# A two-layer transformer block on one core: the first layer's last conditioning vector loaded during the first mixer, four more FFN column blocks by seven products, and one fixed order from the mixer's output into the FFN

## The chip, the core and the metric

The kernel runs on one core of a Trainium2 chip, in one launch. A core has five engines with instruction streams of their own: TensorE (PE, with its weight loads shown apart as PEld), VectorE (DVE), ScalarE (ACT), GpSimd (POOL) and SyncE (SP), which here issues the loads from device memory. Each engine works through its stream in order and waits on semaphores of the others. The metric is the device time of the launch in microseconds (us), smaller is better.

## The reference, cut to what matters

All in float32: 512 tokens, width 1024, two layers. Layer 0 mixes the tokens with a gated linear recurrence (`hgrn2_mixer`), layer 1 with dilated attention. Each mixer is followed by a SwiGLU feed-forward network (FFN) with inner width 2816.

```python
cond = jax.nn.silu(c)
for layer in range(DEPTH):                               # DEPTH = 2
    mod = (cond @ ada_w[layer] + ada_b[layer])[:, None, :]      # 1024 -> 6 * 1024
    sh1, sc1, g1, sh2, sc2, g2 = jnp.split(mod, 6, axis=-1)
    u = rms_norm(h, norm_g[layer, 0]) * (1.0 + sc1) + sh1
    y = hgrn2_mixer(u, ...) if layer % N_MIXERS == 0 else dilated_attention_mixer(u, ...)
    h = h + (1.0 + g1) * rms_norm(y, norm_g[layer, 1])
    u = rms_norm(h, norm_g[layer, 2]) * (1.0 + sc2) + sh2
    gate, up = jnp.split(u @ ffn_w_in[layer], 2, axis=-1)       # 1024 -> 2 * 2816
    y = (jax.nn.silu(gate) * up) @ ffn_w_out[layer]             # 2816 -> 1024
    h = h + (1.0 + g2) * rms_norm(y, norm_g[layer, 3])
```

The six vectors of a layer are called (layer, 0) to (layer, 5) below; (0, 5) is `g2` of layer 0, which is needed only after the first FFN.

## The kernel before, in words

**Split operands.** Every large product is taken in three passes: each operand is kept as a high part and a low part, and `three` (L400 to L404) adds high·high, low·high and high·low into one PSUM bank. ACT makes a high part by a copy into the reduced format, DVE makes the low part by a subtraction. A matmul covers 128 rows of the contraction and up to 512 columns.

**The stream of weights.** One list `items` fixes the order in which all weights are loaded and split (class `Stream`). An item lands in a tile "raw" of 1 MB, of which there are two; SP issues the load of the next item as soon as a raw tile has been read for the last time. Items of kind "w" are split by ACT (L83) and DVE (L84), or piecewise by `pieces` (L104, L105). Items "ada" are quarters of a conditioning vector's weights: vectors (0, 2) to (0, 4) go through PE (`ada_groups`, L221, with the tile `tiled_cond`), all others through DVE as one multiplication and seven multiply-adds for each half (L241, L243) and a sum across partitions on POOL (L245). Items "rows" carry bias and norm rows and finish a gate vector (`row_fin`, L290, L291). Items "quarters" are the four quarters of an FFN block. `weave` mixes the conditioning items into the weights. Before the change (0, 5) stands among the first eight FFN weights.

**The FFN.** The 2816 inner columns are 22 blocks of 128. `PLAIN` gives the number of pairs of blocks that are computed plainly: four in layer 0 and two in layer 1. A plain block takes 48 matmuls of 512 columns for gate and up together. The other blocks go through `seven_products`: by a seven-product scheme over a 2 x 2 cut of weights and tokens, a block takes seven runs of twelve matmuls with 256 columns each. That needs four sums of quarters of the FFN's input, split into `th` and `tl`; `token_sums` makes them: on DVE four additions (L711), four further combinations (L712 to L715) and four subtractions (L718), on ACT four copies (L717).

**Mixer output and entry into the FFN.** `mixer_out` multiplies by the mixer's output weights, normalises (class `Turn`: `gated`, `r_y` and `r_h` for the reciprocal roots on POOL, `upds` for the residual, `xn`, `flip` for the transposes on PE, `u_of` and `parts_of` for the split FFN input `uh`, `ul`), and starts the first pair of plain blocks, two token halves one after the other (`half`; the second half's first lines are L670 and L673). Its four PSUM banks `pss` are handed to `ffn`, where SiLU on ACT (L876) reads two of them and a multiplication on DVE (L877) the other two. The next pair uses the same four banks of tag "mm" again: its first matmul waits for the first SiLU of the pair before, in both programs.

**What sets the order.** Inside `tc.manual_schedule` the instructions of PE, ACT, DVE and POOL keep the written order. Elsewhere a scheduler places them. The last part of `mixer_out` and all of `seven_products` stand in such blocks; what `ffn` does between the two is placed by the scheduler, which may put it between instructions of the fixed blocks.

Of the kernel before, what the change touches and what calls it, by code (L numbers as in the profile page):

```python
# [15 lines left out]
P = 128  # L16
S = 512
# [133 lines left out]
def block_kernel(tc, x, c, positions, ada_w, ada_b, norm_g, hgrn_w_in, lower, hgrn_norm_g, hgrn_w_out,  # L151
# [6 lines left out]
    with ExitStack() as ctx:  # L158
# [14 lines left out]

        pre = ctx.enter_context(ExitStack())
# [34 lines left out]
        tiled_cond = []  # L209
        by_pe = lambda l, v: l == 0 and v in (2, 3, 4)  # L210

        def ada_groups(l, v, hf, kq):


            def run(raw):
                if kq == 0:
                    accs[l, v, hf] = bank("mm")
                ps, r = accs[l, v, hf], V4(raw)
                for k in range(4):
                    j = slice(32 * k, 32 * k + 32)  # L220
                    pe.matmul(ps[j], tiled_cond[0][:, kq * 4 + k], r[:, k], start=kq == 0, stop=kq == 1,  # L221
                              tile_position=(0, 32 * k))
                if kq == 1:
                    accs[l, v, hf] = acc_place()
                    act.copy(accs[l, v, hf], ps)
            return run
# [84 lines left out]


# [29 lines left out]
        PLAIN = (4, 2)  # L342
# [10 lines left out]
        items += weave(hg, ada_seq((0, 2), (0, 4), (0, 3)), 1)  # L353
        items += hg_o
        f0a, f0b = ffn_ws(0)
        n0 = 2 * PLAIN[0]
        items += weave(f0a[:n0], ada_seq((0, 5)), 2, 1) + f0a[n0:]
# [61 lines left out]
        turns = ctx.enter_context(ExitStack())  # L419

# [84 lines left out]
        def mixer_out(oT, otp, groups, gate, l, side, close, tail=None):  # L505
# [69 lines left out]
            n = Turn(side, y0, y1, gate, (l, 1))  # L575

            with tc.manual_schedule(engines=ORDERED):
                (hi_a, lo_a), (hi_b, lo_b) = st.pieces(2)
                n.sq_y(0, 0)
                n.gated(0, 0)  # L580
                mm(0, range(8) if tail is None else (7,))
                n.sq_y(0, 1)
                n.gated(0, 1)
                n.r_y(0)
                n.sq_y(1, 0)
                n.gated(1, 0)
                n.sq_y(2, 0)
                n.upds(0)
                n.sq_y(3, 0)
                n.gated(2, 0)  # L590
                n.r_h(0)
                hi_a()
                n.xn(0)
                mm(1, range(8))
                n.sq_y(1, 1)
                n.gated(1, 1)
                n.r_y(1)
                n.gated(3, 0)
                hi_b()
                n.upds(1)  # L600
                lo_a()
                mm(2, range(4))
                n.flip(0, [bank("b"), bank("b")])
                n.u_of(0, 0)
                n.r_h(1)
                n.u_of(0, 1)
                n.parts_of(0, 0)
                n.xn(1)
                n.parts_of(0, 1)
                lo_b()  # L610
                st.fill()
                mm(3, range(4))
                (hi_a, lo_a), (hi_b, lo_b) = st.pieces(2)
                mm(2, range(4, 6))
                n.flip(1, [bank("b"), bank("b")])
                n.u_of(1, 0)
                n.u_of(1, 1)
                n.parts_of(1, 0)
                n.parts_of(1, 1, dve)
                mm(2, range(6, 8))  # L620
                n.sq_y(2, 1)
                n.gated(2, 1)
                n.r_y(2)
                hi_a()
                n.upd(2, 0)
                mm(3, range(4, 8))
                n.sq_y(3, 1)
                n.sq_h(2, 0)
                n.upd(2, 1)
                n.sq_h(2, 1)  # L630
                hi_b()
                n.gated(3, 1)
                n.r_y(3)
                n.r_h(2)
                lo_a()
                n.xn(2)
                fw = [st.take(0), st.take(0)]
                pss = [bank("mm") for _ in range(4)]

                def half(i, th, kts):  # L640
                    block(*fw[i // 2], (i % 2) * P, 256, pss[i], slice(th * 256, (th + 1) * 256), kts)
                half(0, 0, range(8))
                half(1, 0, range(8))
                n.flip(2, [bank("b"), bank("b")])
                n.upds(3)
                n.u_of(2, 0)
                n.u_of(2, 1, (0, 1))
                n.r_h(3)
                n.u_of(2, 1, (2, 3))
                n.xn(3)  # L650
                n.parts_of(2, 0)
                n.parts_of(2, 1)
                lo_b()
                st.fill()
                half(2, 0, range(8))
                n.flip(3, [bank("b"), bank("b")])
                n.u_of(3, 0)
                n.u_of(3, 1)
                n.parts_of(3, 0)
                n.parts_of(3, 1, dve)  # L660
                half(3, 0, range(8))
                for hi_f, lo_f in st.pieces(2):
                    hi_f()
                    lo_f()
                st.fill()
                tok = slice(256, S)
                for kt in range(KT):
                    a = kt * 256
                    for m, w in enumerate(fw[0]):
# [1066 lines left out]
```

## Time and profile before

| | |
|---|---|
| median of 3 runs | 1527.47 us (1527.37 to 1529.67) |
| the profiled execution | 1527.97 us |
| its span, first to last instruction | 1526.3 us |
| mean granted TensorE clock | 0.998 |
| first FFN, plain part after the entry | 339.24 to 404.55 us of the span |
| second FFN, first matmul of its second pair of blocks | 1202.55 us |

Rows of the timeline give start and duration in us, engine, line, operation, output and inputs, shape, a count, and in brackets the idle time of the engine just before, with what ended it. Rows of windows give for a stretch of the span the busy time and number of instructions of PE, PEld, DVE, ACT and POOL in this order, then the granted clock, the share of the DMA engines and GB/s. Neighbouring matmuls overlap in these records, so a matmul's cost is the distance between starts, not its duration.

### The profile page before, as it was taken

How to read it: one execution, taken by the hardware profiler on the slowest of the kernel's cores; microseconds unless marked ns; L12 is line 12 of the kernel's file. 1: busy time of each engine (PE TensorE's matmuls, PEld its weight loads, DVE VectorE, ACT ScalarE, POOL GpSimd, SP SyncE). 2: the span in 40 equal slices, each digit the busy share in tenths (PEclk: the TensorE clock that was granted, in tenths of full speed). 3: DMA queues.
4: the chain of work that ended last, by engine and by line, in shares of the span. 5: the costliest groups of instructions: out<-in, count | busy, mean ns of one | idle time of the engine just before them, and what ended most of it. 6: DMA issues, size and time to landing. Idle time of an engine off the chain costs nothing.

```text
span 1526.3 us, 22515 instructions
## 1 busy us (share of the span) xinstructions
PE 1507.9 (99%) x8871; PEld 1322.7 (87%) x8871; DVE 1010.5 (66%) x1737; ACT 685.2 (45%) x1091; POOL 233.3 (15%) x204
## 2 busy tenths in 40 slices
PE   8999999999999999999999999999999999999998
PEld 6777888898899988889888888988888999999886
DVE  4587866487688887462567686335656868888633
ACT  4433443362344533362456664245645534444231
POOL 1011210031122211140010111010002212221100
PEclk9999999999999999999999999999999999999999
DMA  9654443126433356414534433443202333334531
GB/s 307 184 160 135 156 138 111 56 84 207 125 109 106 108 198 221 151 55 139 165 99 133 130 111 111 138 111 84 83 30 82 106 89 110 104 107 151 186 117 55
DMA packets 203352, 192.77 MB, mean 126 GB/s; under 512 B 6584, under 2 KB 162416, under 8 KB 203248
## 3 DMA queue, kind: packets, MB, share of 16 engines
q1 hardware_dynamic: 201712, 190.87, 40.6%
q8 instruction: 69, 1.13, 0.3%
q0 software_dynamic: 1024, 0.13, 0.2%
q10 hardware_dynamic: 512, 0.35, 0.1%
q14 instruction: 35, 0.29, 0.1%
HBM read 189.17 MB, written 2.16 MB: 125 GB/s over the span
## 4 chain that ended last, share of the span: by engine, by line
PE 90%; DVE 3%; ACT 2%; issue 2%; DMA 1%; POOL 1%; DVEq 0%; POOLq 0%; ACTq 0%
PE ps_mm L402 20%; PE ps_mm L404 20%; PE ps_mm L403 20%; PE ps_b L402 3%; PE ps_b L404 3%; PE ps_b L403 3%; PE ps_a L404 3%; PE ps_a L403 3%; PE ps_a L402 3%; PE ps_mm L1140 1%; PE ps_a L1140 1%; PE ps_mm L221 1%; PE ps_a L1587 1%; PE ps_b L1140 1%; PE ps_a L1569 1%
## 5 line engine op out<-in xcount | busy, mean ns | idle before, releaser
L402 PE MATMUL ps_mm<-uh,hi 128*128 128x512 f32 (+1 forms) x816 | 309.8, 380 | 0.0
L404 PE MATMUL ps_mm<-uh,lo 128*128 128x512 f32 (+1 forms) x816 | 308.3, 378 | 0.0
L403 PE MATMUL ps_mm<-ul,hi 128*128 128x512 f32 (+1 forms) x816 | 307.4, 377 | 0.0
L84 DVE TENSOR_TENSOR lo<-raw,hi 128x2048 fp32r<-128x2048 f32 x78 | 186.0, 2384 | 168.0 <-ACT hi L83 167.8
L83 ACT CAST hi<-raw 128x2048 fp32r<-128x2048 f32 x78 | 148.8, 1908 | 172.0 <-DMA raw<-in_ffn_w_out_dram 53.4
L402 PEld LDWEIGHTS ps_mm<-uh,hi 128*128 128x128 f32 x816 | 153.8, 188 | 35.2 <-issue 8.4
L404 PEld LDWEIGHTS ps_mm<-uh,lo 128*128 128x128 f32 x816 | 153.8, 188 | 27.2
L403 PEld LDWEIGHTS ps_mm<-ul,hi 128*128 128x128 f32 x816 | 153.8, 189 | 26.2
L402 PE MATMUL ps_mm<-hi,oh 128*128 128x512 f32 x240 | 94.0, 392 | 0.0
L403 PE MATMUL ps_mm<-lo,oh 128*128 128x512 f32 x240 | 93.5, 390 | 0.0
L243 DVE SCALAR_TENSOR_TENSOR shared<-raw,cond,shared 128x512 f32<-128x512 f32 x98 | 73.4, 749 | 29.1 <-DMA raw<-in_ada_w_dram 27.4
L770 ACT CAST hiq<-raw 128x1024 fp32r<-128x1024 f32 x64 | 64.4, 1050 | 62.8 <-DVE raw L758 62.8
L245 POOL PARTITION_ALL_REDUCE shared<-shared x14 | 47.5, 3396 | 288.7 <-DVE shared L243 288.6
L404 PE MATMUL ps_mm<-hi,ul 128*128 128x512 f32 x192 | 76.0, 396 | 0.0
L403 PE MATMUL ps_mm<-lo,uh 128*128 128x512 f32 x192 | 75.9, 396 | 0.0
L774 DVE TENSOR_TENSOR loq<-raw,hiq 128x1024 fp32r<-128x1024 f32 x64 | 75.5, 1220 | 0.6 <-ACT hiq L770 0.6
L402 PE MATMUL ps_mm<-hi,uh 128*128 128x512 f32 x192 | 74.6, 396 | 0.0
L404 PE MATMUL ps_mm<-hi,ol 128*128 128x512 f32 x176 | 68.5, 389 | 0.0
L754 POOL TENSOR_TENSOR raw<-raw 128x512 f32<-128x512 f32 x32 | 52.5, 1642 | 99.4 <-DVE spare L750 42.4
L758 DVE TENSOR_TENSOR raw<-raw 128x1024 f32<-128x1024 f32 x32 | 39.2, 1226 | 36.7 <-POOL raw L754 36.5
L402 PE MATMUL ps_a<-hi,oh 128*128 128x512 f32 x152 | 59.7, 392 | 0.0
L403 PE MATMUL ps_a<-lo,oh 128*128 128x512 f32 x152 | 59.2, 390 | 0.0
(403 smaller groups left out, 3716.0 us busy)
## 6 DMA issues: line engine op xcount, KB each, us to landing
raw<-in_ada_w_dram SPq DMA_DIRECT2D x40, 1024.0 KB, 5.2
raw<-in_ffn_w_in_dram SPq DMA_DIRECT2D x128, 256.0 KB, 4.3
raw<-in_attn_w_in_dram SPq DMA_DIRECT2D x48, 512.0 KB, 4.9
raw<-in_ffn_w_out_dram SPq DMA_DIRECT2D x22, 1024.0 KB, 4.8
raw<-in_hgrn_w_in_dram SPq DMA_DIRECT2D x12, 1024.0 KB, 5.6
raw<-in_ffn_w_in_dram SPq DMA_DIRECT2D x12, 1024.0 KB, 5.1
raw<-in_attn_w_in_dram SPq DMA_DIRECT2D x12, 1024.0 KB, 5.2
first<-in_ada_w_dram SPq DMA_DIRECT2D x14, 512.0 KB, 7.6
```

Source lines behind the costliest of these rows:

```text
L83: self.nc.scalar.copy(hi, t)
L84: self.nc.vector.tensor_sub(lo, t, hi.bitcast(F32))
L243: dve.scalar_tensor_tensor(a, r[:, k], sc, a, op0=OP.mult, op1=OP.add)
L245: pool.partition_all_reduce(a, a, P, bass.bass_isa.ReduceOp.add)
L402: pe.matmul(ps, ah, bh, start=start, stop=False)
L403: pe.matmul(ps, ah, bl, start=False, stop=False)
L404: pe.matmul(ps, al, bh, start=False, stop=stop)
L754: pool.tensor_add(r[:, 2], r[:, 2], r[:, 0])
L758: dve.tensor_tensor(r[:, 0:2], r[:, 0:3:2], r[:, 1:2].broadcast_to((P, 2, 512)), op=OP.add)
L770: act.copy(hi, src)
L774: dve.tensor_sub(lo, src, hi.bitcast(F32))
L1140: pe.matmul(vbanks[hf, t], a, w, start=e == 0 and which == 0, stop=e == KT - 1 and which == 2)
```

## The change

There are three edits. The tile of the replicated conditioning input, made at the very start, is kept until the mixer's end, so that `tiled_cond` and its DVE instruction go. The four loads of vector (0, 5) and its DVE and POOL work move from the first FFN into the last part of the first mixer and its output weights; its two finishing items follow the four FFN weights. `PLAIN` becomes two pairs in layer 0 too, so blocks 4 to 7 go through seven products. And one fixed order now reaches from the last part of `mixer_out` to the start of `seven_products`, in both layers; in it `token_sums` stands ahead of the first pair's SiLU, and `xn(2)` ahead of `r_y(3)` and `lo_a`.

```diff
+        tcx = ctx.enter_context(ExitStack())
+        cond_tiles = tcx.enter_context(tc.tile_pool(name="tiled", bufs=1, side="right")).tile([P, KT, 32], F32, name="cond_tiles")
...
-                    pe.matmul(ps[j], tiled_cond[0][:, kq * 4 + k], r[:, k], start=kq == 0, stop=kq == 1,
+                    pe.matmul(ps[j], cond_tiles[:, kq * 4 + k], r[:, k], start=kq == 0, stop=kq == 1,
...
+        def ada_halves(l, v):
+
+            return [[ada_item(l, v, hf, kq)] for hf in range(2) for kq in range(2)], [fin_item(l, v, hf) for hf in range(2)]
...
-        PLAIN = (4, 2)
+        PLAIN = (2, 2)
...
-        items += weave(hg, ada_seq((0, 2), (0, 4), (0, 3)), 1)
-        items += hg_o
+        gate_loads, gate_fins = ada_halves(0, 5)
+        items += weave(hg, ada_seq((0, 2), (0, 4), (0, 3)) + gate_loads[:2], 1, 0.85)
+        items += weave(hg_o, gate_loads[2:], 0)
         f0a, f0b = ffn_ws(0)
         n0 = 2 * PLAIN[0]
-        items += weave(f0a[:n0], ada_seq((0, 5)), 2, 1) + f0a[n0:]
+        items += f0a[:n0] + gate_fins + f0a[n0:]
...
+        fixed = ctx.enter_context(ExitStack())
...
-            with tc.manual_schedule(engines=ORDERED):
+            fixed.enter_context(tc.manual_schedule(engines=ORDERED))
...
                 n.sq_h(2, 1)
                 hi_b()
+            n.r_h(2)
                 n.gated(3, 1)
+            n.xn(2)
                 n.r_y(3)
-                n.r_h(2)
                 lo_a()
-                n.xn(2)
...
                     tl = qp.tile([P, 4, 4, 256], F32R, name=f"tl{l}")
+                    token_sums(th, tl, midt[:, NF - 8:])
                     for j in range(PLAIN[l]):
...
                             dve.tensor_mul(mid(2 * j + k), pss[2 + k], sg)
-                        if j == 0:
-                            token_sums(th, tl, midt[:, NF - 8:])
+                    fixed.close()
                     seven_products(range(2 * PLAIN[l], NF), mid, sgp, spare, th, tl)
...
-        tiled_cond.append(sc.tile([P, KT, 32], F32, name="tiled_cond"))
-        dve.tensor_scalar(tiled_cond[0], cond.unsqueeze(2).broadcast_to((P, KT, 32)), 1.0 / 32, None, op0=OP.mult)
...
         cx.close()
+        tcx.close()
```

How the built programs differ is shown at three places. Line numbers of the changed program are its own (its L725 is L717 of the listing above, L885 is L876, L719 to L723 are L711 to L715, L754, L758, L766 and L770 are L746, L750, L758 and L762, L483 is L475).

ACT where layer 0 enters its FFN, before: `hi` is the high part of the third FFN weight, `sg` the SiLU of the first pair of blocks, `th` the high parts of the token sums.

```order
L104 CAST hi_2916<-raw_2655 128x8x128 x2
L876 ACT_TABLE_LOAD
L876 ACTIVATE sg_3041<-ps_mm_2754 128x512
L876 ACTIVATE sg_3044<-ps_mm_2755 128x512
L717 CAST th_3039<-mid_3029 128x1024 x2
L83 CAST hi_3069<-raw_2922 128x2048
L717 CAST th_3039<-mid_3029 128x1024
L876 ACTIVATE sg_3201<-ps_mm_3088 128x512
```

The same place of the same engine in the changed program:

```order
L104 CAST hi_2944<-raw_2683 128x8x128 x2
L725 CAST th_3067<-mid_3057 128x1024 x4
L885 ACT_TABLE_LOAD
L885 ACTIVATE sg_3085<-ps_mm_2782 128x512
L885 ACTIVATE sg_3088<-ps_mm_2783 128x512
L83 CAST hi_3091<-raw_2780 128x2048
L885 ACTIVATE sg_3213<-ps_mm_3113 128x512
```

All four `th` copies have moved ahead of the table load and of both SiLUs of the first pair.

ACT where layer 1 enters its FFN, in the changed program (`spare` is the high part of the first quarters item):

```order
L104 CAST hi_10438<-raw_10177 128x8x128 x2
L754 CAST spare_10559<-raw_10444 128x1536
L725 CAST th_10562<-mid_10552 128x1024 x4
L885 ACT_TABLE_LOAD
L885 ACTIVATE sg_10580<-ps_mm_10276 128x512
```

And DVE at that place, in the changed program:

```order
L507 TENSOR_TENSOR ul<-u_10405,uh 128x4x128
L105 TENSOR_TENSOR lo_10439<-raw_10177,hi_10438 128x8x128 x2
L719 TENSOR_TENSOR mid_10552<-uh,ul 128x1024 x4
L720 TENSOR_TENSOR mid_10552<-mid_10552 128x1024
L758 TENSOR_TENSOR spare_10560<-raw_10444,spare_10559 128x1536
L721 TENSOR_TENSOR mid_10552<-mid_10552 128x1024
L722 SCALAR_TENSOR_TENSOR mid_10552<-mid_10552 128x1024
L766 TENSOR_TENSOR raw_10444<-raw_10444 128x1024
L723 SCALAR_TENSOR_TENSOR mid_10552<-mid_10552 128x1024
```

Before, ACT's table load and first SiLU followed `hi` directly in layer 1 as well; now the first quarters item's split (L754, L758) and its sum (L766, behind a POOL addition) also stand among the token sums, ahead of the SiLU.

DVE in the last part of `mixer_out`, layer 0, in the changed program:

```order
L469 SCALAR_TENSOR_TENSOR h<-yg_2586,rr_2742,h 128x512
L469 SCALAR_TENSOR_TENSOR h<-yg_2738,rr_2742,h 128x512
L457 TENSOR_SCALAR rv_2767<-hs_2760 128x1
L453 TENSOR_TENSOR yg_2771<-ps_a_2685,gate_1017 128x512
L483 TENSOR_SCALAR xn_2773<-h,rr_2769 128x1024
L457 TENSOR_SCALAR rv_2775<-ss_2583 128x1
L105 TENSOR_TENSOR lo_2699<-raw_2461,hi_2698 128x8x128
L469 SCALAR_TENSOR_TENSOR h<-yg_2628,rr_2777,h 128x512
```

`xn` (for the third 128 tokens) now stands ahead of the `rv` for the fourth 128 tokens and ahead of the split `lo`; before, it followed both, and the update `h` of the fourth 128 tokens came directly behind it. In layer 1 two of the four first token sums, which the scheduler had put ahead of the third update there, no longer stand in this part.

206 lines of the change are left out of this document (102 added, 104 removed).

## The prediction

> **What bounds the kernel now.** I read the page's busy shares first, then the chain of waits, then windows and the timeline of PE for the gaps.
>
> ```profile
> PE 1507.9 (99%) x8871; PEld 1322.7 (87%) x8871; DVE 1010.5 (66%) x1737; ACT 685.2 (45%) x1091; POOL 233.3 (15%) x204
> PE 90%; DVE 3%; ACT 2%; issue 2%; DMA 1%; POOL 1%; DVEq 0%; POOLq 0%; ACTq 0%
> ```
>
> PE is busy for 1507.9 of 1526.3 us and carries 90% of the chain that ends last. So work taken off PE counts in full, a gap on PE counts in full, and work of other engines counts only where PE comes to wait for it. Three gaps bear on this change:
>
> ```profile
> 76.51 1.06 PE L221 MATMUL ps_mm<-raw,tiled_cond 128*32 128x512 f32 x8 [1.33 <-DVE tiled_cond L1300]
> 319.98 1.09 PE L481 MATMUL ps_b<-ident,xn 128*128 128x128 f32 x8 [0.83 <-DVE xn L475]
> 1183.29 0.88 PE L481 MATMUL ps_b<-ident,xn 128*128 128x128 f32 x6 [2.06 <-DVE xn L475]
> ```
>
> **Part 1, seven products for blocks 4 to 7 (-3.4 us).** The pitch of a matmul comes from two windows, one with only plain blocks and one with only seven products:
>
> ```profile
> 339.45:400.00 60.55, 60.55 (x268) 50.13 (x267) 39.21 (x38) 17.70 (x15) 7.78 (x3) 1.00 0.59 183
> 409.50:550.00 140.50, 140.50 (x1175) 139.00 (x1174) 118.38 (x134) 66.50 (x86) 30.34 (x27) 1.00 0.39 115
> ```
>
> 60.55 / 267 = 0.2268 us at 512 columns (267 loads, one matmul being cut by the edge), 140.5 / 1175 = 0.1196 us at 256. A plain block costs 48 x 0.2268 = 10.89 us, a block by seven products 84 x 0.1196 = 10.05, so four blocks save 4 x 0.84 = 3.4 us. DVE is busy for 118.4 of 140.5 us there, so four more such blocks are not bound by it.
>
> **Part 2, the replicated tile kept (-1.3).** The first gap above waits for one small DVE instruction behind the copies of v_tok. With the tile made at the start, the whole 1.33 us goes; the weights that these matmuls read were issued at 69.67 and a load of that kind lands in 5.2, hence just before the gap.
>
> ```profile
> 69.67 0.37 SPq L65 DMA_DIRECT2D raw<-in_ada_w_dram  x1
> raw<-in_ada_w_dram SPq DMA_DIRECT2D x40, 1024.0 KB, 5.2
> ```
>
> **Part 3, vector (0, 5) in the mixer (+1.0, from 0 to +3).** It brings two multiplications and fourteen multiply-adds to DVE, 14 x 0.749 + 2 x 0.485 = 11.5 us, into the stretch of some 30 us ahead of the mixer's output:
>
> ```profile
> L243 DVE SCALAR_TENSOR_TENSOR shared<-raw,cond,shared 128x512 f32<-128x512 f32 x98 | 73.4, 749 | 29.1 <-DMA raw<-in_ada_w_dram 27.4
> L241 DVE TENSOR_SCALAR shared<-raw,cond 128x512 f32<-128x512 f32 x14 | 6.8, 485 | 14.3 <-DMA raw<-in_ada_w_dram 14.3
> 236.00:266.00 30.00, 30.00 (x202) 25.74 (x201) 15.07 (x20) 13.30 (x22) 0.97 (x1) 1.00 0.33 118
> ```
>
> DVE has 14.9 us free there and DMA two thirds, so it fits, but only just. DVE works in order: a multiply-add now stands between state updates and between the splits of the mixer's output, for which PE comes soon. The floor is 0, the ceiling four of them in a row at one place (3 us). I take a little more than one, 1.0. What goes from the first FFN there had no gap of PE to close, hence 0; the two finishing items ride on DVE while PE computes the second pair.
>
> **Part 4, the order inside the mixer's output (+0.8 and -0.5).** In layer 0 the third `xn` waited for a root on POOL, which came behind another:
>
> ```profile
> 314.26 0.55 POOL L451 TENSOR_TENSOR rr<-rv,expo 128x1 f32<-128x1 f32 x1 [1.42 <-DVE rv L449]
> 317.12 2.02 POOL L451 TENSOR_TENSOR rr<-rv,expo 128x1 f32<-128x1 f32 x2 [2.32 <-DVE rv L449]
> 317.52 1.21 DVE L105 TENSOR_TENSOR lo<-raw,hi 128x1024 fp32r<-128x1024 f32 x1
> 319.18 0.75 DVE L475 TENSOR_SCALAR xn<-h,rr 128x1024 f32<-128x1024 f32 x1 [0.44 <-POOL rr L451]
> 319.84 1.41 DVE L461 SCALAR_TENSOR_TENSOR h<-yg,rr,h 128x512 f32<-128x512 f32 x2
> 323.04 0.75 DVE L475 TENSOR_SCALAR xn<-h,rr 128x1024 f32<-128x1024 f32 x1
> 323.85 0.98 PE L481 MATMUL ps_b<-ident,xn 128*128 128x128 f32 x7
> ```
>
> With its root first (0.55 us from about 317.75) `xn(2)` starts at 318.3, and PE's transposes at 319.1 instead of 320.0: 0.8 gained. But the fourth root now begins behind `xn(2)`, at 319.35, beside the split `lo`. Two roots beside a split took 2.02, so I give this one 1.4; it ends at 320.75. The update of the fourth tokens starts then instead of at 319.84, and `xn(3)` and its transposes come 0.8 to 0.9 us later, while PE is ready earlier. What is late next is thus `xn(3)`: net +0.8, with -0.8 as the other bound. In layer 1 the two token sums that stood in the way go as well; by the same steps `xn(2)` is 2.2 us earlier, PE's gap of 2.06 closes, and `xn(3)`, last again, is 0.5 us earlier than before (bounds -2.1 and -0.3).
>
> **Part 5, the token sums ahead of the first SiLU (+6.0 and +10.0).** This is the large term. The next pair's first matmul waits for the first SiLU, which frees its bank. On ACT that SiLU now stands behind four `th` copies, which wait for DVE's eight sums. Layer 0 before:
>
> ```profile
> 328.18 0.97 DVE L499 TENSOR_TENSOR ul<-u,uh 128x512 fp32r<-128x512 f32 x1 [0.69 <-ACT uh L498]
> 329.25 3.50 DVE L711 TENSOR_TENSOR mid<-uh,ul 128x1024 f32<-128x1024 f32 x3
> 328.05 1.99 ACT L104 CAST hi<-raw 128x1024 fp32r<-128x1024 f32 x2
> 330.83 1.28 ACT L876 ACT_TABLE_LOAD   x1 [0.79 <-PE ps_mm L673]
> 332.13 0.60 ACT L876 ACTIVATE sg<-ps_mm 128x512 f32<-128x512 f32 x1
> 339.24 0.40 PE L402 MATMUL ps_mm<-uh,hi 128*128 128x512 f32 x1
> ```
>
> The SiLU ended at 332.7, seven us before PE needed the bank at 339.24. In the new order, on the same clock: DVE is free at 329.15, makes two `lo` pieces (2.3 us, as in the row at 1194.64 below) to 331.5, then eight sums of 128x1024 at (3.50 - 1.22) / 2 = 1.14 each. The seventh, which the first copy needs, ends at 339.5, the eighth at 340.6. Four copies on ACT, one each 0.95 (two in 1.99), run to 343.4, the table load to 344.7, the SiLU to 345.3. PE is done at 339.24 and waits 6.0 us (5 to 7). Behind the SiLU nothing else is late: the fourth weight's split needs the next 10.9 us of PE's work, which it has.
>
> Layer 1 has in addition the first quarters item among the sums:
>
> ```profile
> 1191.47 0.97 DVE L499 TENSOR_TENSOR ul<-u,uh 128x512 fp32r<-128x512 f32 x1 [0.69 <-ACT uh L498]
> 1194.64 2.35 DVE L105 TENSOR_TENSOR lo<-raw,hi 128x1024 fp32r<-128x1024 f32 x2
> 1202.66 1.48 ACT L746 CAST spare<-raw 128x1536 fp32r<-128x1536 f32 x1 [1.50 <-DMA raw<-in_ffn_w_in_dram]
> 1206.10 1.75 DVE L750 TENSOR_TENSOR spare<-raw,spare 128x1536 fp32r<-128x1536 f32 x1
> 1207.93 3.34 POOL L754 TENSOR_TENSOR raw<-raw 128x512 f32<-128x512 f32 x1 [16.04 <-DVE spare L750]
> 1211.31 1.23 DVE L758 TENSOR_TENSOR raw<-raw 128x1024 f32<-128x1024 f32 x1 [1.18 <-POOL raw L754]
> 1218.61 1.29 POOL L754 TENSOR_TENSOR raw<-raw 128x512 f32<-128x512 f32 x1 [7.33 <-DVE loq L750]
> 1202.55 0.40 PE L402 MATMUL ps_mm<-uh,hi 128*128 128x512 f32 x1
> ```
>
> DVE: free at 1192.4, `lo` to 1194.7, five sums to 1200.4. The quarters land 5.7 us after `lo` frees their tile (1202.66 against 1197.0 before), now at 1200.4; ACT splits to 1201.9, DVE to 1203.6, two sums to 1205.9. Then POOL's addition from 1203.6 on takes 1.29 (the row at 1218.61) or 3.34 (at 1207.93, beside DVE): L758's sum ends at 1207.1 or 1208.2, the last token sum at 1208.2 or 1209.3. Two copies, table load and SiLU add 1.9 + 1.3 + 0.6 = 3.8: 1212.0 or 1213.1. PE is done at 1202.55 and waits 9.5 to 10.5 us; I take 10.0.
>
> [...]
>
> **Part 6, the clock after these gaps (+3.4, from 0 to +6.8).** The only stretch of the trace with a lower clock follows a thin one:
>
> ```profile
> 12.00:14.90 2.90, 1.32 (x13) 1.27 (x13) 1.20 (x6) 2.76 (x6) 0.55 (x1) 1.00 1.09 351
> 14.90:18.40 3.50, 3.41 (x14) 2.72 (x15) 3.43 (x7) 2.06 (x4) 1.79 (x2) 0.51 1.15 323
> 18.40:20.00 1.60, 1.60 (x11) 1.42 (x10) 1.50 (x4) 1.33 (x3) 0.00 (x0) 1.00 1.16 312
> 1180.00:1184.00 4.00, 1.95 (x17) 1.74 (x16) 3.43 (x7) 1.61 (x4) 1.74 (x2) 1.00 0.00 0
> ```
>
> With PE busy for 1.32 of 2.9 us, the clock was halved for about 3.4 us; with 1.95 of 4.0 it was not. The new gaps of 6 and 10 us are emptier than both. At half speed 3.4 us of work takes 3.4 us and yields half: 1.7 us lost for each gap, 3.4 together. The floor is no halving, the ceiling twice the stretch.
>
> [...]
>
> **The sum.** -3.4 - 1.3 + 1.0 + 0.8 - 0.5 + 6.0 + 10.0 + 3.4 = +16.0 us. The profiled execution took 1527.97, half a microsecond above the median of 1527.47; all terms are differences, so I add them to the median: 1543.5, or 1.0% slower.
>
> **The rivals.**
> - *The gaps come, the clock stays full.* For it: the gap of 2.06 us left the clock at 1.00. Against it: 14.9 to 18.4. Without the 3.4 the time is 1540.
> - *The mixer is held back too.* A multiply-add waits in DVE's order for its load, and state updates and splits queue behind it. For it: DVE's 27.4 us of waits for such loads in L243's row. Against it: DMA is at a third there. One landing of 5.2 us that PE comes to feel gives about 1548.
> - *Not slower: the sums are hidden.* If the eight sums and four copies end before PE's half pass does, the SiLU is in time and Part 5 and Part 6 vanish, while both `xn` gaps close: -3.4 - 1.3 - 0.8 - 2.1 = -7.6, 1520. It decides from the point where the copies end at 337.3 (339.24 less 1.9 for table load and SiLU) instead of 343.4. For it only a start of the sums well ahead of `ul`; against it, they read the last `ul`, which ends at 329.15, and 2.3 + 9.1 = 11.4 us of DVE work lie behind that.
> - *The seven products save nothing.* At 256 columns the weight loads are nearly the bound (139.0 of 140.5 us). Against it: the pitch of 0.1196 already holds them. It would give 1547.
>
> **How the numbers follow.** Forecast 0.63; full clock 0.18; mixer held back 0.07; products without gain 0.03; hidden sums 0.05; gaps about half as long, 1531 to 1536, 0.04. Within 0.2%, 3 us, is what a measurement of this kernel can't tell from no change; that needs both gaps to be almost gone. So faster 0.06, same 0.02, slower 0.92. The low end, 1534, takes no halving, gaps of 5 and 8.5 and the better bounds of Part 4: -4.7 - 2.9 + 13.5 = +5.9. The high end, 1550, takes gaps of 6.5 and 10.5, a doubled halving and +3 in the mixer, less a little, since these do not all come together. Only the hidden sums, part of the half gaps and a tail above lie outside.
>
> **What would show it.** In the changed profile PE's first 512-column matmul after each second-half pass should follow a gap of about 6 and 10 us put down to ACT's SiLU (`sg`), with ACT's `th` copies just before that. The granted clock should fall to about 0.5 for some 3.4 us behind each. L221's first group should have no gap; the transposes of `xn(2)` none to speak of, those of `xn(3)` 1.5 to 2 us in both layers. Plain 512-column matmuls of the first FFN should be 192 fewer, 256-column ones 336 more. Were the two gaps under 2 us, Part 5 would be wrong, and with it the sign.

## The result and the profile after

The changed kernel takes 1550.2 us (median of 4 runs, 1549.8 to 1551.6) against 1528.2 for the kernel before: 1.0145 times as long, 95% interval 1.0127 to 1.0162. The direction was forecast, the size was not: 1543.5 was forecast, with a range up to 1550. The profiled execution spans 1548.1 us against 1526.3.

The page of the changed kernel, first the busy times, then the chain of waits:

```profile
PE 1511.3 (98%) x9015; PEld 1331.8 (86%) x9015; DVE 1033.9 (67%) x1764; ACT 694.8 (45%) x1107; POOL 239.2 (15%) x212
PE 86%; DVE 5%; ACT 3%; issue 3%; DMA 2%; POOL 1%; SPq 0%; POOLq 0%; DVEq 0%; ACTq 0%
```

PE's share of the chain fell from 90% to 86%: PE is busy for only 3.4 us more, and waits more. The view of waits of PE, with the sum in us, the number and the longest, says for whom:

```profile
PE ps_mm L408 <- ACT sg L885: 17.0, 2, 10.8
PE ps_a L1428 <- DVE aT L1421: 3.5, 1, 3.5
PE ps_b L489 <- DVE xn L483: 3.0, 2, 1.5
```

The first row is the pair of gaps that the forecast turned on, the third the two late transposes it named. The second is a gap it does not have. The timeline of PE gives their places (start, duration, operation, and in brackets the idle time ahead):

```profile
75.26 1.06 PE L222 MATMUL ps_mm<-raw,cond_tiles 128*32 128x512 f32 x8
277.78 1.08 PE L1428 MATMUL ps_a<-ident,aT 128*128 128x128 f32 x4 [3.49 <-DVE aT L1421]
323.49 1.04 PE L489 MATMUL ps_b<-ident,xn 128*128 128x128 f32 x8
329.01 1.09 PE L489 MATMUL ps_b<-ident,xn 128*128 128x128 f32 x8 [1.50 <-DVE xn L483]
350.79 0.79 PE L408 MATMUL ps_mm<-uh,hi 128*128 128x512 f32 x1 [6.23 <-ACT sg L885]
1190.00 1.04 PE L489 MATMUL ps_b<-ident,xn 128*128 128x128 f32 x8
1195.56 1.09 PE L489 MATMUL ps_b<-ident,xn 128*128 128x128 f32 x8 [1.50 <-DVE xn L483]
1221.87 0.79 PE L408 MATMUL ps_mm<-uh,hi 128*128 128x512 f32 x1 [10.77 <-ACT sg L885]
```

The windows around the three gaps (length, busy times of PE, its weight loads, DVE, ACT and POOL, then granted clock, DMA share, GB/s):

```profile
277.20:280.70 3.50, 2.92 (x15) 2.95 (x15) 1.12 (x2) 0.69 (x1) 0.00 (x0) 0.51 0.00 0
348.90:355.80 6.90, 5.01 (x12) 3.95 (x13) 5.80 (x6) 4.10 (x4) 0.00 (x0) 0.51 0.00 0
1215.90:1226.20 10.30, 4.33 (x10) 3.46 (x11) 10.30 (x10) 9.77 (x10) 0.00 (x0) 0.50 0.00 1
```

At each gap the clock is halved, from within the gap into the work behind it. PE's 512-column matmuls start 0.43 us apart there (from 352.24 on), against 0.23 at full clock (from 355.96 on), so about half of PE's busy time there is lost: 1.5, 2.5 and 2.2 us.

Following one PE instruction after another through both traces (these are the landmarks spoken of below) gives how far the changed kernel lags at each place, and the steps between the places are the terms of the forecast:

| Step | Forecast, us | Measured, us |
|---|---|---|
| replicated tile kept | -1.3 | -1.25 |
| vector (0, 5) in the mixer | +1.0 | +5.8 |
| order in the mixer's output, layer 0 | +0.8 | +0.6 |
| entry to the first FFN | +6.0 | +6.4 |
| clock behind it, and seven products | +1.7 - 3.4 | -2.0 |
| attention | 0 | -0.6 |
| order in the mixer's output, layer 1 | -0.5 | -0.5 |
| entry to the second FFN | +10.0 | +10.9 |
| clock behind it | +1.7 | +2.1 |
| sum | +16.0 | +21.4 |

The spans differ by 21.8 us; the 0.4 that the steps leave lie behind the last matmul. One step is far off: the mixer. Here is what stands ahead of its new gap, from the timelines of POOL and DVE of the changed kernel:

```profile
265.19 3.33 DVE L405 TENSOR_TENSOR oT<-oT,oh 128x512 fp32r<-128x512 f32 x2
265.45 3.52 POOL L246 PARTITION_ALL_REDUCE shared<-shared  x1 [16.80 <-DVE shared L244]
271.85 0.15 DVE L422 TENSOR_SCALAR rv<-oss 128x4 f32<-128x4 f32 x1
275.85 1.05 POOL L423 TENSOR_TENSOR orr<-rv,expo 128x4 f32<-128x4 f32 x1 [6.88 <-issue]
276.94 0.69 DVE L1421 TENSOR_TENSOR aT<-ps_b,orr 128x512 f32<-128x512 f32 x1 [3.83 <-POOL orr L423]
```

PE's transposes need `aT`, which needs the seventh head's root `orr` from POOL. The root's input `rv` is ready at 272.0, yet the root starts at 275.85, and its idle time is put down to "issue": POOL waits for nothing that the profile shows. What it has just done is the all-reduce of vector (0, 5), which ended at 268.97, 6.9 us earlier. The same all-reduce also lies beside two splits on DVE that take 3.33 us together. In the kernel before, with no all-reduce near, the same root starts 0.1 us behind its input, which is ready at 268.04:

```profile
268.18 1.01 POOL L417 TENSOR_TENSOR orr<-rv,expo 128x4 f32<-128x4 f32 x1 [31.20 <-DVE rv L416]
269.22 0.69 DVE L1416 TENSOR_TENSOR aT<-ps_b,orr 128x512 f32<-128x512 f32 x1 [0.56 <-POOL orr L417]
```

### The profile page after: what moved, and what is told of

Read it like the earlier page. It is cut to its first block, busy times and chain, and to the rows that moved or that the text cites. A ratio compares the mean times of both kernels' runs of the same rounds, so it can differ in the third digit from the quotient of the medians.

```text
span 1548.1 us, 22922 instructions
## 1 busy us (share of the span) xinstructions
PE 1511.3 (98%) x9015; PEld 1331.8 (86%) x9015; DVE 1033.9 (67%) x1764; ACT 694.8 (45%) x1107; POOL 239.2 (15%) x212
## 4 chain that ended last, share of the span: by engine, by line
PE 86%; DVE 5%; ACT 3%; issue 3%; DMA 2%; POOL 1%; SPq 0%; POOLq 0%; DVEq 0%; ACTq 0%
PE ps_mm L408 19%; PE ps_mm L410 19%; PE ps_mm L409 19%; PE ps_b L408 3%; PE ps_b L410 3%; PE ps_b L409 3%; PE ps_a L409 3%; PE ps_a L410 3%; PE ps_a L408 3%; PE ps_mm L1148 1%; ACT junk L444 1%; PE ps_a L1148 1%; PE ps_a L1593 1%; PE ps_a L1575 1%; PE ps_mm L222 1%
## 5 line engine op out<-in xcount | busy, mean ns | idle before, releaser
L408 PE MATMUL ps_mm<-uh,hi 128*128 128x512 f32 (+1 forms) x752 | 286.6, 381 | 17.0 <-ACT sg L885 17.0
L84 DVE TENSOR_TENSOR lo<-raw,hi 128x2048 fp32r<-128x2048 f32 x74 | 176.9, 2390 | 162.7 <-ACT hi L83 162.5
L410 PE MATMUL ps_mm<-uh,lo 128*128 128x512 f32 (+1 forms) x752 | 285.0, 379 | 0.0
L409 PE MATMUL ps_mm<-ul,hi 128*128 128x512 f32 (+1 forms) x752 | 284.2, 378 | 0.0
L408 PEld LDWEIGHTS ps_mm<-uh,hi 128*128 128x128 f32 x752 | 142.8, 190 | 50.7 <-ACT sg L885 17.4
L410 PEld LDWEIGHTS ps_mm<-uh,lo 128*128 128x128 f32 x752 | 142.7, 190 | 25.2
L409 PEld LDWEIGHTS ps_mm<-ul,hi 128*128 128x128 f32 x752 | 142.9, 190 | 24.2
L782 DVE TENSOR_TENSOR loq<-raw,hiq 128x1024 fp32r<-128x1024 f32 x72 | 84.7, 1217 | 0.4 <-ACT hiq L778 0.4
L762 POOL TENSOR_TENSOR raw<-raw 128x512 f32<-128x512 f32 x36 | 57.8, 1607 | 135.5 <-DVE spare L758 74.8
L766 DVE TENSOR_TENSOR raw<-raw 128x1024 f32<-128x1024 f32 x36 | 44.1, 1225 | 42.1 <-POOL raw L762 42.1
L812 POOL TENSOR_TENSOR shared<-shared 128x256 f32<-128x256 f32 x36 | 27.7, 769 | 211.6 <-DVE shared L811 211.6
L408 PE MATMUL ps_mm<-th,hiq 128*128 128x256 f32 x216 | 59.8, 277 | 0.0
```

Source lines behind the costliest of these rows:

```text
L84: self.nc.vector.tensor_sub(lo, t, hi.bitcast(F32))
L408: pe.matmul(ps, ah, bh, start=start, stop=False)
L409: pe.matmul(ps, ah, bl, start=False, stop=False)
L410: pe.matmul(ps, al, bh, start=False, stop=stop)
L762: pool.tensor_add(r[:, 2], r[:, 2], r[:, 0])
L766: dve.tensor_tensor(r[:, 0:2], r[:, 0:3:2], r[:, 1:2].broadcast_to((P, 2, 512)), op=OP.add)
```

## The experiments

Each is told by its edit to the changed kernel or, where it says so, to the kernel before. Ratios are to the kernel before on the same chip.

**1. Sums behind both SiLUs.**

```
-                    token_sums(th, tl, midt[:, NF - 8:])
 ...
+                        for k in range(2):
+                            act.activation(sgs[k], pss[k], AF.Silu)
+                        if j == 0:
+                            token_sums(th, tl, midt[:, NF - 8:])
+                        for k in range(2):
+                            dve.tensor_mul(mid(2 * j + k), pss[2 + k], sgs[k])
```

> The changed kernel with the token sums moved behind the first pair's two SiLUs, in the same fixed order; nothing else is moved. Theory (the two gaps of 6.2 and 10.8 us ahead of the second pair, and the halved clock of 2.5 and 2.1 us behind them, are all the work of the sums standing ahead of the SiLU): 1550.2 - 21.6 = 1528.6, bounds 1527 to 1531. The second pair's first matmul follows the half passes without a gap in both layers, and the granted clock stays at 1.0 from 345 to 360 and from 1210 to 1230. The gap of 3.5 us at 277 stays. Rival (the clock falls for another reason than the gap): the gaps go, the halved stretches stay, 1533.

Measured: 1538.6 us, 1.0062 (1.0046 to 1.0077). Only 11.6 of the 21.6 us came back, which is neither the theory's time nor the rival's. The long gaps are gone, but in the second FFN two others stand in their place:

```profile
1219.35 0.47 PE L408 MATMUL ps_mm<-uh,hi 128*128 128x512 f32 x1 [2.40 <-DVE mid L888]
1222.06 0.79 PE L410 MATMUL ps_mm<-uh,lo 128*128 128x512 f32 x1 [2.00 <-DVE lo L84]
```

In a fixed order the sums are ahead of something wherever they stand: here of the products `mid`, which free the second pair's banks, and of the split of that pair's last weight. A third new wait, of 0.9 us, comes late in the first FFN (at 538) and is for the split of a quarters item. The clock was halved again behind the two gaps, for 6.8 us, and in the mixer for 6.8 us instead of 3.4.

**2. The all-reduces moved to the first FFN.**

```
-                if kq == 1:
+                if kq == 1 and (l, v) != (0, 5):
                     pool.partition_all_reduce(a, a, P, bass.bass_isa.ReduceOp.add)
 ...
-        items += f0a[:n0] + gate_fins + f0a[n0:]
+        items += f0a[:n0 - 1] + [reduce_item(0, 5, hf) for hf in range(2)] + f0a[n0 - 1:n0] + gate_fins + f0a[n0:]
```

> The changed kernel with the two all-reduces over partitions for vector (0, 5) moved from the mixer's output into the first FFN, behind the first pair's products; loads and multiply-adds stay in the mixer. Theory (the all-reduce at 265.45 makes the normalizing root on POOL start 3.8 us late and stretches two splits on DVE by 2.1): PE's gap of 3.5 us at 277 and the 1.7 us of halved clock go, 1545.0, bounds 1544 to 1547. Rival (the sixteen multiplications and multiply-adds on DVE hold the root back): the gap stays at 3 us or more, 1550. Second rival: the late all-reduces hold back the first FFN's finishing items or POOL's first weight sum, and 1548 to 1552 come out with a new gap after 355.

Measured: 1549.7 us, 1.0139 (1.0125 to 1.0152). The time is the second rival's, though without its new gap after 355, and the mixer did what the theory says. Its rows on DVE and POOL:

```profile
264.66 1.47 DVE L412 TENSOR_TENSOR oT<-oT,oh 128x512 fp32r<-128x512 f32 x2
269.77 0.16 DVE L429 TENSOR_SCALAR rv<-oss 128x4 f32<-128x4 f32 x1
270.08 1.57 POOL L430 TENSOR_TENSOR orr<-rv,expo 128x4 f32<-128x4 f32 x1 [31.78 <-DVE rv L429]
```

With all multiply-adds still in place and only the all-reduce gone, the two splits take 1.47 us instead of 3.33, the root starts 0.2 us behind its input, and PE has no gap there. Of the 5.1 us that the mixer won, 4.5 were lost at the first FFN's entry, as the timelines of POOL, DVE and PE show:

```profile
333.56 7.09 POOL L317 PARTITION_ALL_REDUCE shared<-shared  x2 [5.55 <-issue]
330.82 6.67 DVE L726 TENSOR_TENSOR mid<-uh,ul 128x1024 f32<-128x1024 f32 x4
337.41 3.33 DVE L727 TENSOR_TENSOR mid<-mid 128x1024 f32<-128x1024 f32 x1
340.78 1.22 DVE L728 TENSOR_TENSOR mid<-mid 128x1024 f32<-128x1024 f32 x1
349.22 0.79 PE L415 MATMUL ps_mm<-uh,hi 128*128 128x512 f32 x1 [10.40 <-ACT sg L892]
```

The two all-reduces now lie beside the token sums: the four additions take 6.67 us instead of 4.62 in the changed kernel, and one further sum takes 3.33 where its neighbour takes 1.22. So the gap that these sums make grows from 6.2 to 10.4 us, and the clock was halved for 13.7 us from 341.4 on. The first row also shows that POOL takes 5.5 us before an all-reduce that has nothing to wait for.

**3. Both edits.**

> Both edits, sums behind the SiLUs and all-reduces in the first FFN. If the two costs are separate and nothing else is lost: 1550.2 - 21.6 - 5.2 = 1523.4, bounds 1522 to 1526, about 0.3% faster than the kernel before. If the all-reduces were hidden behind the gap of the first FFN in the run with one edit only, they show here, with 1526 to 1530.

Measured: 1536.8 us, 1.0051 (1.0038 to 1.0063), well off the 1523.4 of two separate costs, and above the other case's 1526 to 1530 too. The all-reduces beside the sums and the sums ahead of the split both remain: PE waits twice for 2.0 us for `lo` and once for 2.0 for `mid`.

**4. The root left out.** For all eight heads; the kernel then computes something else, and only its time is of use.

```
-            rstd_of(r, ss, P, cp, 4)
+            rv = fresh(cp, [P, 4], "rv", 2)
+            dve.tensor_scalar(rv, ss, 1.0 / P, EPS, op0=OP.mult, op1=OP.add)
+            dve.tensor_copy(r, rv)
```

> The changed kernel with the mixer's normalizing root left out: a copy on DVE stands where POOL's root stood, for all eight heads, so that nothing of this chain runs on POOL; all-reduces and multiply-adds stay where they are. It tells what is POOL's share of the lateness at 277. Theory (3.8 us of the lateness of 7.7 are POOL's late start after the all-reduce, and 3.9 us had been slack): the transposes at 277 have no gap, 1545, bounds 1544 to 1547. Rival (DVE's lateness alone is what PE feels): a gap of 2 us or more stays, 1548 to 1550.

Measured: 1544.7 us, 1.0107 (1.0093 to 1.0121), as the theory has it. The rows on DVE:

```profile
263.52 3.33 DVE L405 TENSOR_TENSOR oT<-oT,oh 128x512 fp32r<-128x512 f32 x2
271.10 0.15 DVE L1422 COPY orr<-rv 128x4 f32<-128x4 f32 x1
271.43 0.68 DVE L1423 TENSOR_TENSOR aT<-ps_b,orr 128x512 f32<-128x512 f32 x1
```

The splits are as slow as in the changed kernel and DVE is as late, but without POOL in the chain `aT` comes at 271.4 instead of 276.9 and PE does not wait. DVE's lateness alone, multiply-adds included, fits into the slack. It is POOL's late start that PE feels.

**5. Sums free.** The fixed order ends with the mixer's output, as before, and the sums stand in the code behind the first pair.

```
             aux.close()
+            fixed.close()
             return pss
 ...
-                    token_sums(th, tl, midt[:, NF - 8:])
 ...
+                        if j == 0:
+                            token_sums(th, tl, midt[:, NF - 8:])
```

> The changed kernel with the fixed order ending at the end of the mixer's output, as before the change, and the token sums in the code behind the first pair; the scheduler places them. Vector (0, 5), the seven products, the tile and the order inside the mixer's output stay. Theory: the whole of the 21.6 us at the two entries goes, also what the run with the sums behind both SiLUs left (waits for the second pair's last weight split and for the products that free the banks). From the landmarks: 1528.2 - 1.3 (tile) + 5.8 (mixer) + 0.6 (order, layer 0) - 4.5 (seven products) - 0.6 (attention) = 1528.2, bounds 1526.5 to 1531. Rival (other work at the entries costs the rest, whatever the order): 1535 to 1539, like the run before.

Measured: 1531.6 us, 1.0023 (1.0014 to 1.0032), 0.6 above the bounds. Of PE's waits the two at the entries are gone; at the top of the list stand

```profile
PE ps_b L489 <- DVE xn L483: 4.2, 3, 1.5
PE ps_a L1429 <- DVE aT L1422: 3.7, 1, 3.7
```

One of the three waits for `xn`, of 1.2 us, is new: in layer 1 the scheduler puts two token sums ahead of the third update again, as in the kernel before. In its trace this run ends 4.1 us behind the kernel before, where the theory had 0. The main parts are 1.5 us of clock in the mixer, where behind the same gap it was halved for 6.8 us in this trace instead of 3.4, 0.9 for the transposes of layer 1, and 1.9 in attention, which stay open. The scheduler's way is to lay sums, splits and products of the pair alternately.

**6. Sums free, all-reduces called later.** The edit of run 5 together with that of run 2, here with the all-reduces called behind the fourth weight.

> The same with the two all-reduces of (0, 5) called in the first FFN, behind the second pair's last weight split. Theory: the mixer's 5.5 to 5.8 us go and the all-reduces meet only token sums that have time: 1522.6, bounds 1521 to 1525, 0.3 to 0.4% faster than the kernel before. Rival (an all-reduce on POOL holds DVE back wherever it stands, as at 336 in the run with both edits, and PE feels it in the first FFN): 1526 to 1530.

Measured: 1532.0 us, 1.0021 (1.0011 to 1.0030): no change, since the edit did not do what it says. Outside a fixed order the scheduler takes the all-reduce as soon as its data is there, and it stands where it stood:

```profile
265.14 3.52 POOL L317 PARTITION_ALL_REDUCE shared<-shared  x1 [17.01 <-DVE shared L244]
275.83 1.05 POOL L430 TENSOR_TENSOR orr<-rv,expo 128x4 f32<-128x4 f32 x1 [7.17 <-issue]
```

**7 and 8. Two single parts, on the kernel before.** Two plain pairs in the first FFN (`PLAIN = (2, 2)`) and nothing else:

> The kernel before with two plain pairs in the first FFN and nothing else of the change. If the work saved counts in full: 1528.2 - 4.5 = 1523.7, bounds 1522.5 to 1525. Rival: vector (0, 5) then has four loads of 1 MB and sixteen multiplications and multiply-adds on DVE in a stretch shorter by 21.8 us, the first quarters item comes late and PE waits ahead of the first seven products: 1528 to 1535.

Measured: 1544.0 us, 1.0102 (1.0089 to 1.0116), slower than even the rival. Ahead of the first seven products PE waits for the first quarters item:

```profile
374.22 0.58 PE L402 MATMUL ps_mm<-uh,spare 128*128 128x256 f32 x1 [12.98 <-ACT spare L746]
```

The four loads of vector (0, 5) stand ahead of that item, and with two plain pairs there is not the time for them. With the vector in the mixer (run 5) this wait does not exist, so with the weights in this order Part 1 pays only together with Part 3. The move alone, with the new item lists and nothing else:

> The kernel before with vector (0, 5) loaded in the mixer and nothing else of the change. Theory (all of the mixer's cost comes from this part): a gap of about 3.5 us ahead of the transposes of the mixer's seventh head near 278, with some 1.7 us of halved clock, 1534, bounds 1531.5 to 1535.5. Rival (the cost needs the tile or the earlier start of the first group as well): 1528 to 1529.5.

Measured: 1535.6 us, 1.0042 (1.0028 to 1.0055). The gap at the seventh head (3.7 us, ahead of L1428) is there, with 6.8 us of halved clock, which puts the time just above its bounds. Behind the mixer PE's lag on the kernel before changes by no more than 0.3 us, so the cost is this part's own.

**9. The second all-reduce between two roots.** On the version with the sums free:

```
+            if hd == NH - 1:
+                dve.tensor_copy(root, r[:, 0:1])
 ...
+            if l == 0:
+                a = accs[0, 5, 1]
+                dve.scalar_tensor_tensor(a[:, 0:1], root, 0.0, a[:, 0:1], op0=OP.mult, op1=OP.add)
+                pool.partition_all_reduce(a, a, P, bass.bass_isa.ReduceOp.add)
```

> The kernel with the free sums (1531.6) with the second all-reduce of (0, 5) tied behind the last head's root by a one-column addition of zero times that root, so that it stands between the last head's root (it ends near 278) and the first root of the mixer's output (at 296). The first all-reduce stays near 245. Theory: POOL needs 5.5 us from an ordinary instruction to an all-reduce, 3.5 for it and 7.0 back, 16 in all, and 18 are there; so the root of the seventh head starts near 269 to 270 again, the gap of 3.7 us and the halved clock behind it (3.4 lost) go, 1524.5, bounds 1523 to 1527. Rival (what holds the root back is DVE's extra work): gap and time stay, 1530 to 1532. Second rival: the way back is longer than the room, and the first transposes of the mixer's output come late, 1526 to 1530.

Measured: 1527.0 us, 0.9989 (0.9980 to 0.9997), at the theory's upper bound. PE's gap at the seventh head is gone; on POOL and DVE:

```profile
277.84 1.01 POOL L424 TENSOR_TENSOR orr<-rv,expo 128x4 f32<-128x4 f32 x1 [5.29 <-DVE rv L423]
285.31 3.25 POOL L587 PARTITION_ALL_REDUCE shared<-shared  x1 [6.46 <-PE ps_a L1436]
285.40 2.69 DVE L1447 TENSOR_TENSOR oT_late<-oT_late,Q 128x512 f32<-128x512 f32 x1 [2.76 <-ACT oT_late L1437]
297.34 0.60 POOL L460 TENSOR_TENSOR rr<-rv,expo 128x1 f32<-128x1 f32 x1 [8.78 <-DVE rv L458]
```

Both ways of POOL fit between the roots. Beside the all-reduce the DVE product takes 2.69 us where 0.69 is usual, and the mixer's output comes 0.9 us later against its own start than in the next run.

**10. No all-reduce.** On the version with the sums free, the partition sums of (0, 5) by ones on PE:

```
-                if kq == 1:
+                if kq == 1 and (l, v) != (0, 5):
                     pool.partition_all_reduce(a, a, P, bass.bass_isa.ReduceOp.add)
 ...
-                if by_pe(l, v):
+                if by_pe(l, v) or (l, v) == (0, 5):
                     b = bank("b")
                     pe.matmul(b, ones, a, start=True, stop=True)
```

> The kernel with the free sums with no all-reduce for (0, 5) at all: the partition sums come from two products with a tile of ones on PE, as those of vector (0, 2) do. Theory: the mixer's gap and its halved clock go as above, PE pays two products of 128x512 at full precision, about 0.9 us each, 1.8: 1526.3, bounds 1524.5 to 1528. Against the run with the all-reduce between the roots it tells whether the all-reduce costs anything there. Rival (DVE's extra work): 1530 to 1533.

Measured: 1525.4 us, 0.9979 (0.9970 to 0.9988): faster than both kernels, 0.2% faster than the one before. The root of the seventh head is back to its input,

```profile
270.18 1.57 POOL L423 TENSOR_TENSOR orr<-rv,expo 128x4 f32<-128x4 f32 x1 [31.81 <-DVE rv L422]
```

and the clock is full from the start to the last few us. Against run 9 it is 1.6 us faster, but not in the stretches that the two edits touch: there it wins 0.9 in the mixer and pays 1.7 for PE's two products in the first FFN. What puts it ahead lies elsewhere (run 9's trace has 3.4 us of halved clock at the start, as the kernel before has, and a longer attention) and stays open.

**11. The sums ahead, alone.** The kernel before with the fixed order and the sums ahead of the first SiLU (and the tile kept), the rest undone.

> Of the change only the token sums ahead of the first SiLU in the fixed order, and the tile kept; four plain pairs, vector (0, 5) in the first FFN and the order inside the mixer's output are as before. Theory (this part alone makes both gaps and the halved clock behind them): 1528.2 - 1.3 + 6.2 + 2.5 + 10.8 + 2.1 = 1548.5, bounds 1545.5 to 1551; by the prediction's own terms for the part, 6.0 + 10.0 + 3.4, it would be 1546.3. Rival (the gaps need the mixer's lateness or the missing plain pairs): 1530 to 1540.

Measured: 1548.6 us, 1.0138 (1.0123 to 1.0153). PE's waits have the two gaps again, 16.3 us together:

```profile
PE ps_mm L407 <- ACT sg L884: 16.3, 2, 10.1
```

The price set by the landmarks, 1548.5, is met to 0.1 us: neither the mixer's lateness nor the missing plain pairs are needed for it. That it is met so closely is luck in part. In its trace the third transposes of layer 1 come 1.5 us earlier, since the fixed order takes two token sums out of their way, which the sum of the price leaves out; and the clock at the first gap was halved for 10.2 us instead of 6.8.

**12. Ones on PE in the changed kernel.** The edit of run 10 with the fixed order and the sums ahead left in.

> The changed kernel as it is, fixed order and sums ahead included, with the all-reduces of (0, 5) replaced by two products with ones on PE. If the mixer's cost and the cost at the two entries only add: 1550.2 less the 6.2 that the same edit gave with the sums free (1531.6 to 1525.4) = 1544.0, bounds 1542.5 to 1546. If the gap at the first FFN's entry takes back what the mixer wins: 1548 to 1550.

Measured: 1545.4 us, 1.0119 (1.0103 to 1.0136), within the bounds. The costs of the mixer and of the entries add; PE's two products fall into the first gap, which is 4.5 us here instead of 6.2.

## Why the prediction was right in direction and wrong in size

- **Part 5, the sums ahead of the SiLU: right.** The gaps of 6.2 and 10.8 us follow the chain that was worked out, in this order in the timelines of DVE and ACT of the changed kernel:

```profile
336.56 4.62 DVE L719 TENSOR_TENSOR mid<-uh,ul 128x1024 f32<-128x1024 f32 x4
344.87 1.23 DVE L723 SCALAR_TENSOR_TENSOR mid<-mid 128x1024 f32<-128x1024 f32 x1
344.94 3.88 ACT L725 CAST th<-mid 128x1024 fp32r<-128x1024 f32 x4 [9.74 <-DVE mid L722]
348.85 1.28 ACT L885 ACT_TABLE_LOAD   x1
350.14 1.09 ACT L885 ACTIVATE sg<-ps_mm 128x512 f32<-128x512 f32 x2
```

  Run 11 shows that this part costs 21.0 us with no more than the tile's gain beside it, run 5 that undoing it alone gives back 18.6 of 22.0. The rivals "hidden" and "half as long" fall with it. In layer 1 the wait came out at the longer end, but not on the way that was worked out:

```profile
1212.35 2.18 POOL L762 TENSOR_TENSOR raw<-raw 128x512 f32<-128x512 f32 x1 [12.05 <-DVE spare L758]
1213.44 2.17 DVE L722 SCALAR_TENSOR_TENSOR mid<-mid 128x1024 f32<-128x1024 f32 x1
```

  POOL's addition took 2.18 us, between the two rows of the forecast, and ended a microsecond before DVE came to need it. What PE felt is the token sum beside it, 2.17 us instead of 1.22. What made that sum longer was not tested.

- **Part 3, vector (0, 5) in the mixer: the step that failed.** The prediction listed "two multiplications and fourteen multiply-adds" and bounded their cost by four multiply-adds in a row, 0 to 3 us. The vector also brings two all-reduces on POOL, and these were put at nothing, without a reason, though they move with it. The part measures 5.8 us: 0.7 by 245 us of the span, a gap of 3.5, and 1.5 of halved clock. The 0.7 is there in run 10 too, which has the multiply-adds and no all-reduce, so of what was costed it is the price, inside its bounds; the rest is the all-reduce's. Run 4 puts the gap on POOL's start behind the all-reduce, run 2 shows that the multiply-adds without it leave no gap, run 8 that the part costs this by itself, runs 9 and 10 that it vanishes when the all-reduce moves away from the root or goes. The rival "the mixer is held back too" had its place and nearly its size (1548), with 7% and by another mechanism: it has a multiply-add wait for its load, and none did that PE felt.

- **Part 6, the clock: right in kind, under-sized.** 4.6 us behind the two gaps instead of 3.4, because the halved stretches were 6.8 and 10.2 us, not 3.4, and reached 5.0 and 4.3 us into PE's work. A third one, behind the mixer's gap, is in Part 3's price. The rival with full clock falls.

- **Part 1, seven products: right, under-sized.** -4.5 us instead of -3.4. The pitch was taken from the window 409.5 to 550 as one with only seven products, and it is not: the FFN's output, with 512 columns, begins at 541.18. The view of windows gives for this end of it

```profile
541.18:550.00 8.82, 8.82 (x41) 7.32 (x40) 6.96 (x11) 4.77 (x7) 1.18 (x1) 1.00 0.40 143
```

  so 41 of the 1175 matmuls are of the longer kind, and the pitch came out too long. Landmarks do not suffer from that: the first seven products' start and the start of the FFN's output, before and after, from PE's timelines.

```profile
404.55 0.28 PE L402 MATMUL ps_mm<-uh,spare 128*128 128x256 f32 x1
541.18 0.40 PE L402 MATMUL ps_mm<-hi,oh 128*128 128x512 f32 x1
```

```profile
375.02 0.28 PE L408 MATMUL ps_mm<-uh,spare 128*128 128x256 f32 x1
550.69 0.40 PE L408 MATMUL ps_mm<-hi,oh 128*128 128x512 f32 x1
```

  136.63 / 14 and 175.67 / 18 are both 9.76 us for a block of 84 matmuls, against the 10.05 that the window gave; four blocks save 4 x (10.89 - 9.76) = 4.5. In the first FFN of run 5, with no gap and full clock, the way from the last transposes to attention is 4.5 us shorter than before. The rival without gain falls.

- **Parts 2 and 4: right**, to 0.2 us in each term: no gap ahead of L222, none ahead of the third transposes, 1.5 us ahead of the fourth in both layers. In layer 1 the gain hangs on the fixed order reaching over the token sums: without it, in run 5, the transposes come 0.9 us later than before instead of 0.5 earlier.

Of the 5.4 us by which the sum fell short, 4.8 are the mixer, 1.3 the gaps, 1.2 the clock; the seven products give back 1.1, and 0.8 lies in attention and the order. That 1550.2 is only just beyond the range says nothing for the mixer's term: its ceiling was 3, and it measures 5.8.

## What to carry to other kernels

When work is moved, list every instruction it issues on every engine before costing any; the one that hurt was the smallest in count, two instructions on an engine that is idle 85% of the time. Ask of each what the next instruction on its engine is and who waits for that: the all-reduce on POOL cost most to the ordinary POOL instruction behind it, which was ready 3.0 us after its end and started 6.9 us after it in the changed kernel. A fixed order that is good at one place should end where its reason ends; and a gap on PE cost here, beyond its length, from 1.5 us of halved clock (the 3.5 us in the changed kernel's mixer) to 3.0 (the 3.7 us in run 5's). A window from which a pitch is taken must hold one kind of matmul alone.

## What the hardware showed that was not expected

POOL took its time between an ordinary instruction and an all-reduce, both ways. From an ordinary instruction to an all-reduce that has nothing to wait for it was 5.5 us (5.55 and 5.51 in runs 2 and 3); in the first FFN's output, where its input came 5 us into this time, it was 7.6 to 8.1 (runs 1, 3 and 7). From an all-reduce back to an ordinary one that is ready, it was 6.9, 7.1, 7.2 and 7.0 us in the changed kernel and runs 5, 6 and 8, where the input came 3 us behind the all-reduce, and 7.0 in run 7, where it came 5.5 us behind (POOL's addition at 377.44); so in these rows the time runs from the all-reduce and not from the input. In the kernel before no ordinary instruction was needed so soon behind an all-reduce (the nearest, at 396.80, comes 16.5 us behind one), so its trace has no row for it. What POOL does in this time no run here shows.

Two-input DVE instructions beside an all-reduce were slower in these rows: by 1.9 us (3.33 for two splits in the changed kernel against 1.47 in run 2), 2.1 (3.33 for a sum against 1.22, both in run 2), 2.1 (6.67 for four additions in run 2 against 4.62 in the changed kernel) and 2.0 (2.69 for a product against 0.69, both in run 9).

The halved clock came in whole steps: between the program's first 20 us and its end, stretches of 3.4, 6.8 and 10.2 us in the changed kernel and of 13.7 us in run 2. In the changed kernel these stretches begin whole multiples of 3.413 us apart: at 14.47, 277.29, 348.97 and 1215.96 us, which are 77, 21 and 254 steps.

So it is not a gap's length alone that counts, but how it falls into these steps. In the changed kernel PE was busy, by its records, for 0.41 us of the step before 277.29 and for 2.92 us of the next, and one step was halved. In run 5, with a gap 0.2 us longer (3.7 against 3.5), it was busy for 0.85, 2.24 and 3.42 us of three steps, and two were halved. Laid over the traces of the kernel before and the changed kernel, the whole steps fall apart as follows. Those in which PE was busy for 0, 0.12, 0.32 and 0.42 of the time in the changed kernel (0.32 at its end, 0.42 from 11.06 on), and for 0.45 (from 11.51 on) and 0 (at its end) in the kernel before, were followed by a halved one; those with 0.50 (from 1130.63 on in the changed kernel) or more were not. The full clock came back after halved steps with 0.80 (from 14.47 on), 0.86 and 1.00 in the changed kernel and 0.97 (from 14.93 on) in the kernel before; it did not after 0, 0.27 and 0.47 in the changed kernel, nor after the 2.24 us of run 5, which are 0.66. With that agree the gaps of 3.5 us in the changed kernel and 4.0 in run 6, which brought 3.4 us, and those of 3.9, 3.7 and 3.7 in runs 1, 5 and 8, which brought 6.8; and a stretch can begin while PE is still idle (at 348.97, with PE starting at 350.8). The gap of 2.06 us in the kernel before, from which the first rival argued, is spread over two steps, with PE busy for 2.37 and 2.40 us, 0.69 and 0.70, and the clock stayed full. In run 7 a gap of 2.04 us at the same place of the program falls into one step, which leaves 1.37 us, 0.40, and the next step was halved. So a step need not be idle to be followed by a halved one.
